# Hybrid decoder step on one core: the samples' recurrent outputs taken from the old state, the state update moved into the MLP phase

## The chip, the cores and the metric

The kernel runs on one core of a Trainium2 chip. The metric is the device time of one execution in microseconds (us). The engines are named as in the profile: PE (TensorE: matmuls), PEld (its weight loads), DVE (VectorE), ACT (ScalarE), POOL (GpSimd, which here also issues DMAs) and SP (whose queue issues the weight loads).

## What is computed

One layer of a decoder for 256 prompt rows and 8 sample rows (one new token each). A mixer with three branches (A: spatial gating, B: HGRN2 recurrence, C: gated linear attention, GLA) is followed by a squared-ReLU MLP. What the change touches is the recurrence of the 8 samples, which have a state S of 128 x dv per head (HGRN2: 8 heads, dv 128; GLA: 4 heads, dv 256):

```python
def gated_linear_recurrence(q, k, v, log_f, s0):
    """S_t = diag(f_t) S_{t-1} + k_t v_t^T ; o_t = S_t^T q_t (per head)."""
...
x = x + gt1 * rmsnorm(out, p['g_post_mix'][l])
h2 = rmsnorm(x, p['g_pre_mlp'][l]) * (1.0 + sc2) + sh2
y2 = jnp.square(jax.nn.relu(h2 @ p['w_mlp_up'][l])) @ p['w_mlp_down'][l]
x = x + gt2 * rmsnorm(y2, p['g_post_mlp'][l])
```

The updated state S_t of each sample is an output of its own; nothing else in the step reads it. The output o_t goes on into the branch's projection. Since a sample has one token, o = S_t^T q can also be had from the old state: o = S_old^T (f q) + (k.q) v.

## The kernel before

All 264 rows go through every weight matrix together. A weight block arrives by a DMA of 512 KB from SP's queue into one of four `raw` tiles (`Stream.load`), ACT casts a half of it to `whi` (L109) and DVE subtracts to make the remainder `wlo` (L106); there are six buffers of each (`SPLIT_BUFS`). PE then runs three matmuls for each 128x128 piece (`granule`, L601 to L603). A granule is 24 such matmuls and uses two `whi`/`wlo` pairs, one for each 12 matmuls; a column of 256 outputs takes four granules in the up projection of the MLP and in `zin`, two in the down projection. At the end of a column ACT or DVE takes the sum out of PSUM (two buffers, `new_acc`).

Everything else runs beside this stream. After each granule `background()` advances one tick: generators in the queue `bg` do the mixer's branches, those in `bs` the samples, each at its `rate`; `slot()` then puts the small PE matmuls that have become ready between two granules. In the mixer phase the order of PE and POOL is that of the code; DVE and ACT are ordered by a scheduler at build time, and each engine executes strictly in its order. In the MLP phase before the change only PE's order was fixed.

The samples' recurrence is `samples_r(G)`, one generator for each of the three groups (two of 4 HGRN2 heads, one of the 4 GLA heads). In its preparation it makes `fs` = f and `qm` (q of each sample, spread over columns of its own). Then, for each of 8 samples (in one step of 4 heads, or in GLA's case two steps of 2 heads):

- `fetch` (L1073) brings the old state into one of 4 `st` tiles; `values` (L1079) brings v, broadcast over the partitions, from the DRAM scratch `vs_d` into one of 2 `vbc` tiles. Both are DMAs that POOL issues;
- ACT multiplies each head by f (L1099), DVE adds k times v (L1101): `st` now is the new state;
- POOL issues its write to the output (L1102);
- `slot()` multiplies the new state by `qm` on PE (L640) and DVE adds the product up in `os` (L103).

When all samples of a group are done, `os` is normalised; `finish(i)` later transposes it into the branch's rows. Beside it `mixer_r` works on the prompt rows of the same group; its products `kd` and `qd` are read by PE at L1220.

Of the kernel before, what the change touches and what calls it, by code (L numbers as in the profile page):

```python
# [11 lines left out]
ALU = mybir.AluOpType  # L12
# [36 lines left out]
SLOT_WAIT = 4  # L49
HELD_OWED = 1.0  # L50
LEVELS_HELD = 3
FETCHED = 3
AGE = 2
ADA_LAND = 4

# [2 lines left out]
def hybrid_step_kernel(  # L58
# [39 lines left out]

    def mul(o, a, b):
        V.tensor_tensor(o, a, b, op=ALU.mult)  # L100

    def add(o, a, b):
        V.tensor_tensor(o, a, b, op=ALU.add)  # L103
# [505 lines left out]
    def slot():  # L609

        lv = [x for x in levels if x[0] + AGE <= now[0]][:2]
        if any(x[3] == 64 for x in lv):
            lv = lv[:1]
        sv = [x for x in samples if x[0] + AGE <= now[0]]
        del levels[:len(lv)]
        del samples[:len(sv)]
        pls, two = [], None
        for _, lhs, rhs, m, _ in lv:
            if m == 64:
                pl = sm([P, 8, 64])  # L620
            else:
                two = two or sm([P, 2, 8, 32])
                pl = two[:, len(pls)]
            pls.append(pl)
            n = max(m, 32)
            for h in range(4):
                for hf in range(2):
                    for b in range(4):
                        if m >= 32 and b // (n // 32) % 2:
                            continue  # L630
                        t0 = hf * P + b * 32
                        q0 = t0 if m < 32 else hf * P + b // (n // 32) * n + n
                        T.matmul(pl[32 * b:32 * b + 32, 2 * h + hf, :], lhs[:, h, t0:t0 + 32], rhs[:, h, q0:q0 + n], start=True, stop=True)  # L633
        if sv:
            G, qm, os_ = sv[0][1]
            nh = 512 // G.dv
            po = sm([P, G.dv])
            for h in range(4):
                for i, (_, _, b, sts) in enumerate(sv):
                    T.matmul(po[32 * h:32 * h + 32, :], qm[:, h, b, :], sts[h // nh][:, h % nh, :], start=i == 0, stop=i == len(sv) - 1)  # L640
        if rounds.due():
            rounds.steps()
        for pl, x in zip(pls, lv):
            x[4](pl)
        if sv:
            if sv[0][2] == 0:
                V.tensor_copy(os_, po)
            else:
                add(os_, os_, po)

    later = []

# [222 lines left out]
    def mixer_a():  # L875
# [30 lines left out]
            add(v, v, lnb)  # L906
            yield

        vs = tmp([P, 8, NS], "vsa", 1)
        w8 = tmp([P, 8, NS], "vsb", 1)  # L910
        r8 = tmp([P, NS], "vsr", 1)
        for i in range(2):
# [66 lines left out]

    att = const([P, 8, P], "att")  # L980
    nc.gpsimd.memset(att, 0.0)
    vs_d = dp.tile([3, 8 * NS, P], F32, tag="vs_d", name="vs_d")

    class Group:
# [73 lines left out]
    def samples_r(G):  # L1058

        dv = G.dv  # L1060
        nj, nh = dv // P, 512 // dv
        q, k, g = G.q, G.k, G.g
        fs = tmp([P, 4, NS], "fs")
        S.activation(fs, g[:, :, NP:NT], AF.Exp)
        qm = blk([P, 4, NS, 32])
        mul(qm, q[:, :, NP:NT].unsqueeze(3).to_broadcast([P, 4, NS, 32]),
            delta.rearrange("p (b c) -> p b c", b=NS).unsqueeze(1).to_broadcast([P, 4, NS, 32]))
        steps = [(b, h) for b in range(NS) for h in range(0, 4, nh)]
        ahead, vals = [], []

        def fetch(b, h):
            st = tmp([P, nh, dv], "st", ST_BUFS)
            nc.gpsimd.dma_start(st, G.s_in(b, h, nh))  # L1073
            ahead.append((st, now[0]))

        def values(b, h):
            v = tmp([P, 4, P], "vbc", VB_BUFS)
            r0 = 4 * nj * b + h * nj
            nc.gpsimd.dma_start(v, vs_d[G.i, r0:r0 + 4, :].partition_broadcast(P))  # L1079
            vals.append((v.rearrange("p (h j) v -> p h (j v)", h=nh), now[0]))  # L1080

        for s in steps[0:2]:
            fetch(*s)
            yield
        values(*steps[0])
        yield
        os_ = tmp([P, dv], f"os{G.i}", 1)
        sts = []
        for n, (b, h0) in enumerate(steps):
            if n + 2 < len(steps):  # L1090

                yield lambda: len(sts) + sum(len(x[3]) for x in samples) <= ST_BUFS - 3
                fetch(*steps[n + 2])
            if n + 1 < len(steps):
                values(*steps[n + 1])
            yield lambda: now[0] >= max(ahead[0][1] + FETCHED, vals[0][1] + FETCHED - 1)
            st, v = ahead.pop(0)[0], vals.pop(0)[0]
            for i in range(nh):
                S.activation(st[:, i, :], st[:, i, :], AF.Copy, scale=fs[:, h0 + i, b:b + 1])  # L1099
            for i in range(nh):  # L1100
                V.scalar_tensor_tensor(st[:, i, :], v[:, i, :], k[:, h0 + i, NP + b:NP + b + 1], st[:, i, :], ALU.mult, ALU.add)  # L1101
            nc.gpsimd.dma_start(G.s_out(b, h0, nh), st)  # L1102
            sts.append(st)
            if h0 + nh == 4:
                samples.append((now[0], (G, qm, os_), b, sts))
                sts = []
            yield
        yield lambda: not samples
        yield READY
        ss, rr = tmp([P, 1], "sss", 1), tmp([P, 1], "srr", 1)  # L1110
        S.activation(tmp([P, dv], "vt"), os_, AF.Square, accum_out=ss)
        rstd_small(ss, 1.0 / dv, rr)
        S.activation(os_, os_, AF.Copy, scale=rr)
        G.os = os_
        yield

    def mixer_r(G):
# [172 lines left out]
                yield 0.6  # L1290
        G.o = o

    def finish(i):
# [114 lines left out]
    gs = tmp([P, KT, NS], "gs", 1)  # L1408

    def gated(m, src, Gv):  # L1410

# [312 lines left out]
    def up(f, zs=()):  # L1724
        ah, al = [], []
        for m in range(FB // CW):
            z = zs[m] if m < len(zs) else linear(w_mlp_up[0], 0, KT, f * FB + m * CW, CW, h2H, h2L)
            rl = tmp([P, 2, NT], "vt")
            S.activation(rl, z, AF.Relu)  # L1729
            if m % 2 == 0:  # L1730
                ah.append(blk(dt=F32R))
                al.append(blk(dt=F32R))
            a, b = pair(ah[-1], m % 2), pair(al[-1], m % 2)
            sq = tmp([P, 2, NT], "gt")
            S.activation(a, rl, AF.Square)  # L1735
            mul(sq, rl, rl)
            sub(b, sq, a.bitcast(F32))
        return tiles(ah), tiles(al)
# [31 lines left out]
    order = tc.manual_schedule(engines={mybir.EngineType.PE})  # L1770
    order.__enter__()
    pend = up(0, zs)
    for f in range(NFB):
        nxt = up(f + 1) if f + 1 < NFB else None
        if f == NFB - 1:
            rounds.drain()
            mul(G2, mod[:, 5 * KT:6 * KT, :], gpost2T.unsqueeze(2).to_broadcast([P, KT, NC]))
# [92 lines left out]
```

## Time and profile before

| | |
|---|---|
| time before, 3 runs | median 1937.72 us, 1937.01 to 1941.59 |
| the profiled execution | 1936.48 us, of which the span of the trace is 1934.7 |
| PE, PEld busy | 1900.5 us, 1811.2 us |
| DVE, ACT, POOL busy | 1191.7 us, 996.9 us, 87.7 us |
| moved by DMA | 442.06 MB |
| samples' recurrence in the trace | from 372.9 us (first fetch) to 845.3 us (last product) |

The times lie along the program like this: start and the first pass over the input projection up to 300 us, the mixer to 1130, the change to the MLP around 1150, the MLP to 1922, and the end. In what follows, a row of the timeline has the start, the duration, the engine, the line and the operation, and in brackets the engine's idle time ahead of it with what ended it. A row of a table by stretches has, for each engine, busy time and number of instructions, then the granted PE clock (1.00 is full), the DMA engines' mean busy share and the GB/s moved.

### The profile page before, as it was taken

The page shows a single profiled execution, that of the slowest core. Times are in us where ns is not written, and L with a number is a line of the kernel's source. Part 1 is how long each engine was busy: PE and PEld are TensorE (multiplying, and loading weights), DVE is VectorE, ACT ScalarE, POOL GpSimd, SP SyncE. Part 2 cuts the span into 40 slices and gives each one's busy share as a digit, 9 for nine tenths or more (in the row PEclk, how much of TensorE's full clock was granted, in tenths as well). Part 3 has the DMA queues.
Part 4 walks back from the last instruction along what each step waited for, and adds up shares of the span by engine and source line. Part 5 has one row for each costly group of instructions (what it writes and reads, how often), then busy time and mean ns, then how long its engine had stood idle before and what let it go on. Part 6 is the DMA issues. An engine that isn't in the chain of part 4 may idle for free.

```text
span 1934.7 us, 42322 instructions
## 1 busy us (share of the span) xinstructions
PE 1900.5 (98%) x17092; PEld 1811.2 (94%) x17092; DVE 1191.7 (62%) x2129; ACT 996.9 (52%) x1812; POOL 87.7 (5%) x144
## 2 busy tenths in 40 slices
PE   7999999998999999999999999999999999999998
PEld 5989999998999998999999999999999999999997
DVE  5666567685577695565555667545555555555666
ACT  4444354664666765544444566454444545454544
POOL 1000000001101112200000010000000000000000
PEclk9999999999999999999999999999999999999999
DMA  9986696777588678987777846776655556565563
GB/s 325 349 319 236 226 307 206 226 254 252 184 269 278 221 260 277 309 264 251 251 252 231 304 143 193 230 239 188 183 178 183 182 179 184 176 184 179 181 183 102
DMA packets 339380, 442.06 MB, mean 228 GB/s; under 512 B 14930, under 2 KB 281024, under 8 KB 339184
## 3 DMA queue, kind: packets, MB, share of 16 engines
q1 hardware_dynamic: 329120, 409.62, 65.6%
q0 software_dynamic: 8992, 28.48, 4.6%
q8 instruction: 134, 2.20, 0.4%
q10 hardware_dynamic: 1072, 1.25, 0.2%
q14 instruction: 62, 0.51, 0.1%
HBM read 427.60 MB, written 11.70 MB: 227 GB/s over the span
## 4 chain that ended last, share of the span: by engine, by line
PE 94%; DVE 2%; DMA 2%; ACT 1%; issue 1%; POOL 0%; SPq 0%; DVEq 0%; ACTq 0%
PE mm L601 29%; PE mm L602 28%; PE mm L603 28%; PE ada L341 3%; PE ada L273 2%; DMA vbc<-vs_d 1%; PE sm L633 1%; DVE wlo L106 1%; PE sm L845 1%; PE sm L640 0%; DMA st<-in_state_gla_dram 0%; DMA b<-in_x_prompt_dram 0%; DVE b L103 0%; DMA b<-in_w_ada_dram 0%; ACT b L109 0%
## 5 line engine op out<-in xcount | busy, mean ns | idle before, releaser
L601 PE MATMUL mm<-b,whi 128*128 128x264 f32 x4592 | 1318.1, 287 | 5.7 <-DVE b L103 2.9
L602 PE MATMUL mm<-b,whi 128*128 128x264 f32 x4592 | 1307.7, 285 | 1.4 <-DVE b L106 1.2
L603 PE MATMUL mm<-b,wlo 128*128 128x264 f32 x4592 | 1305.1, 284 | 3.1 <-DVE wlo L106 2.6
L106 DVE TENSOR_TENSOR wlo<-raw,whi 128x512 fp32r<-128x512 f32 x1136 | 770.3, 689 | 498.0 <-ACT whi L109 495.4
L109 ACT CAST whi<-raw 128x512 fp32r<-128x512 f32 x1132 | 692.3, 618 | 726.9 <-PE mm L602 648.2
L601 PEld LDWEIGHTS mm<-b,whi 128*128 128x128 f32 x4592 | 865.4, 188 | 49.2 <-issue 24.7
L603 PEld LDWEIGHTS mm<-b,wlo 128*128 128x128 f32 x4592 | 865.5, 188 | 3.7 <-DVE wlo L106 3.7
L602 PEld LDWEIGHTS mm<-b,whi 128*128 128x128 f32 x4592 | 865.5, 188 | 2.4 <-DVE b L106 1.3
L103 DVE TENSOR_TENSOR b<-b,mm 128x528 f32<-128x528 f32 (+1 forms) x137 | 95.7, 700 | 98.2 <-PE mm L603 98.2
L1101 DVE SCALAR_TENSOR_TENSOR st<-vbc,b,st 128x128 f32<-128x128 f32 (+1 forms) x96 | 34.2, 391 | 54.7 <-DMA vbc<-vs_d 49.8
L1099 ACT ACTIVATE st<-st,fs 128x128 f32<-128x128 f32 (+1 forms) x96 | 37.0, 430 | 58.7 <-DMA st<-in_state_hgrn_dram 32.5
L273 PE MATMUL ada<-b,cT 128*32 128x256 f32 (+1 forms) x640 | 34.7, 354 | 6.9 <-DMA b<-in_w_ada_dram 6.8
L341 PE MATMUL ada<-araw,cT 128*32 128x512 f32 x296 | 39.9, 601 | 0.0
L273 PEld LDWEIGHTS ada<-b,cT 128*32 128x32 f32 x640 | 17.8, 112 | 18.8 <-ACT b L234 6.1
L100 DVE TENSOR_TENSOR b<-b,b 128x512 f32<-128x512 f32 (+1 forms) x47 | 34.1, 742 | 1.4 <-ACT b L1209 0.9
L1102 POOL DMA_DIRECT2D out_dram<-st x32 | 23.5, 735 | 156.4 <-DVE st L1101 155.6
L341 PE MATMUL ada<-b,cT 128*32 128x512 f32 x216 | 25.8, 593 | 0.0
L106 DVE TENSOR_TENSOR b<-gt,b 128x528 fp32r<-128x528 f32 x32 | 22.7, 708 | 3.6 <-ACT whi L109 0.5
L106 DVE TENSOR_TENSOR b<-b 128x1024 f32<-128x1024 f32 (+1 forms) x24 | 24.3, 1018 | 0.0
L100 DVE TENSOR_TENSOR gt<-vt 128x528 f32<-128x528 f32 x32 | 22.5, 702 | 0.9 <-ACT vt L1729 0.9
L1735 ACT ACTIVATE b<-vt 128x528 fp32r<-128x528 f32 x32 | 20.7, 647 | 1.0
L341 PEld LDWEIGHTS ada<-b,cT 128*32 128x32 f32 x216 | 6.9, 110 | 15.1 <-issue 14.6
(385 smaller groups left out, 882.6 us busy)
## 6 DMA issues: line engine op xcount, KB each, us to landing
raw<-in_w_in_dram SPq DMA_DIRECT2D x232, 512.0 KB, 4.6
raw<-in_w_mlp_up_dram SPq DMA_DIRECT2D x128, 512.0 KB, 3.7
raw<-in_w_mlp_down_dram SPq DMA_DIRECT2D x128, 512.0 KB, 3.6
b<-in_w_ada_dram SPq DMA_DIRECT2D x102, 512.0 KB, 6.3
araw<-in_w_ada_dram SPq DMA_DIRECT2D x74, 512.0 KB, 5.4
raw<-in_w_branch_dram SPq DMA_DIRECT2D x48, 512.0 KB, 4.3
raw<-in_w_out_dram SPq DMA_DIRECT2D x32, 512.0 KB, 4.2
b<-in_w_ada_dram SPq DMA_DIRECT2D x32, 256.0 KB, 6.5
```

Source lines behind the costliest of these rows:

```text
L100: V.tensor_tensor(o, a, b, op=ALU.mult)
L103: V.tensor_tensor(o, a, b, op=ALU.add)
L106: V.tensor_tensor(o, a, b, op=ALU.subtract)
L109: S.copy(hi, src)
L273: T.matmul(acc[32 * j:32 * j + 32, 0:n], cT[:, k, :], w[:, n * j:n * j + n], start=k == 0, stop=k == KT - 1)
L341: T.matmul(self.acc[32 * j:32 * j + 32, :], cT[:, k, :], ws[j // 2][:, j % 2 * 512:j % 2 * 512 + 512], start=k == 0, stop=k == KT - 1)
L601: T.matmul(o, a, xh(k + j), start=first and j == 0, stop=False)
L602: T.matmul(o, a, xl(k + j), start=False, stop=False)
L603: T.matmul(o, b, xh(k + j), start=False, stop=last and j == n - 1)
L1099: S.activation(st[:, i, :], st[:, i, :], AF.Copy, scale=fs[:, h0 + i, b:b + 1])
L1101: V.scalar_tensor_tensor(st[:, i, :], v[:, i, :], k[:, h0 + i, NP + b:NP + b + 1], st[:, i, :], ALU.mult, ALU.add)
L1102: nc.gpsimd.dma_start(G.s_out(b, h0, nh), st)
```

## The change

`samples_r` no longer updates the state. It forms f q instead of q for `qm`, multiplies the old state by it as it lands, and starts `os` with (k.q) v: v and the products k q are put into a padded tile `pads` and transposed on PE (four transposes in all), k q is summed over the partitions by one small matmul per group, and ACT scales. The fetched states rotate through the 4 `st` and the 2 `vbc` tiles; POOL issues neither `values` nor the writes in the mixer phase. f and k of all groups are kept in `kept`.

A new generator `states()` does the update in the MLP phase: it fetches each of the 32 steps' state a second time, with v beside it, and works in half steps (2 heads, or in GLA's case 1). Each half step waits until a column has been taken out of PSUM: POOL copies one element per partition of that column (the token), then the factors f and k that the half step needs, and ACT and DVE then do their operation as before. The write of a step is issued behind the next token. There are 65 tokens, one for each column from the up projection of the MLP's second block on. POOL's order is now fixed in that phase too.

```diff
-FETCHED = 3
+FETCHED = 4
+UPDATE_RATE = 9.0
...
-        fs = tmp([P, 4, NS], "fs")
+        fs, ks = (kept[:, G.i, c].rearrange("p (h b) -> p h b", h=4) for c in range(2))
...
+            odd = fetched[0] % 3 == 2
+            fetched[0] += 1
+            st = tmp([P, nh, dv], "vbc" if odd else "st", VB_BUFS if odd else ST_BUFS)
             nc.gpsimd.dma_start(st, G.s_in(b, h, nh))
...
+            T.transpose(ps, pads.rearrange("p h b -> p (h b)"), ident)
+            S.copy(os_[:, j * P:(j + 1) * P], ps)
...
+        mul(pads[:, :, 0:NS], q[:, :, NP:NT], ks)
+        mul(qf, q[:, :, NP:NT], fs)
...
+        T.matmul(ps[:, 0:1], pads.rearrange("p h b -> p (h b)"), ones[:, 0:1], start=True, stop=True)
...
+        S.activation(os_, os_, AF.Copy, scale=kq)
...
-            for i in range(nh):
-                S.activation(st[:, i, :], st[:, i, :], AF.Copy, scale=fs[:, h0 + i, b:b + 1])
-            for i in range(nh):
-                V.scalar_tensor_tensor(st[:, i, :], v[:, i, :], k[:, h0 + i, NP + b:NP + b + 1], st[:, i, :], ALU.mult, ALU.add)
-            nc.gpsimd.dma_start(G.s_out(b, h0, nh), st)
...
+        def token():
+            nc.gpsimd.tensor_copy(tmp([P, 16], "sa")[:, 0:1], paced[0])
+            paced[0] = None
...
+            for half in range(2):
+                yield lambda: paced[0] is not None
+                token()
+                hs = range(half * nh // 2, (half + 1) * nh // 2)
+                fk = tmp([P, 16], "sx")[:, 0:nh].rearrange("p (c i) -> p c i", c=2)
+                nc.gpsimd.tensor_copy(fk, kept[:, G.i].rearrange("p c (h b) -> p c h b", h=4)[:, :, h + hs[0]:h + hs[-1] + 1, b])
+                write()
+                for j, i in enumerate(hs):
+                    S.activation(st[:, i, :], st[:, i, :], AF.Copy, scale=fk[:, 0, j:j + 1])
+                    V.scalar_tensor_tensor(st[:, i, :], v[:, i, :], fk[:, 1, j:j + 1], st[:, i, :], ALU.mult, ALU.add)
+                if half == 0 and n + 1 < len(todo):
+                    fetch(*todo[n + 1])
...
             S.activation(rl, z, AF.Relu)
+            paced[0] = rl[:, 0, 0:1]
...
                     add(dst[:, i, :], dst[:, i, :], z[:, i, :])
+            paced[0] = dst[:, 0, 0:1]
```

DVE's order in the mixer phase, first group, around the last states of the group, before the change (`wlo` is a weight's remainder, L1101 the update of a state, L100 the product `qd` that PE reads at L1220):

```order
L106 TENSOR_TENSOR wlo_6084<-raw_5942,whi_6083 128x512
L1101 SCALAR_TENSOR_TENSOR st_5860<-vbc_6104,b_4817,st_5860 128x128 x3
L106 TENSOR_TENSOR wlo_6088<-raw_5942,whi_6087 128x512
L1101 SCALAR_TENSOR_TENSOR st_5860<-vbc_6104,b_4817,st_5860 128x128
L1101 SCALAR_TENSOR_TENSOR st_6102<-vbc_6115,b_4817,st_6102 128x128 x2
L106 TENSOR_TENSOR wlo_6146<-raw_5987,whi_6145 128x512
L1101 SCALAR_TENSOR_TENSOR st_6102<-vbc_6115,b_4817,st_6102 128x128
L1340 SCALAR_TENSOR_TENSOR b_5868<-gt_6056,mm_6058 128x528
L106 TENSOR_TENSOR wlo_6150<-raw_5987,whi_6149 128x512
L1101 SCALAR_TENSOR_TENSOR st_6102<-vbc_6115,b_4817,st_6102 128x128
L106 TENSOR_TENSOR wlo_6182<-raw_6021,whi_6181 128x512
L100 TENSOR_TENSOR b_6094<-b_6094,b_581 128x512
```

The same place after the change (L107 and L101 are the old L106 and L100, L104 the old L103, L1395 the old L1340):

```order
L107 TENSOR_TENSOR b_6051<-b_656 128x1024
L104 TENSOR_TENSOR os_888_5109<-os_888_5109,sm_5994 128x128
L101 TENSOR_TENSOR b_6051<-b_6051,b_4818 128x1024
L107 TENSOR_TENSOR wlo_6042<-raw_5903,whi_6041 128x512
L101 TENSOR_TENSOR b_6052<-b_6052,b_581 128x512
L107 TENSOR_TENSOR wlo_6046<-raw_5903,whi_6045 128x512
L107 TENSOR_TENSOR wlo_6089<-raw_5941,whi_6088 128x512
L1395 SCALAR_TENSOR_TENSOR b_5827<-gt_6014,mm_6016 128x528
```

The updates are gone from between the weights' remainders, and the product that PE reads at L1220 stands right behind the first remainder instead of behind eight updates and four remainders of later blocks.

POOL's order for the same group before the change, from the fourth fetch (`st` from the input is a fetch, `vbc` the values, `out_dram` a write):

```order
L1073 DMA st_5460<-in_state_hgrn_dram 128x4x128
L1079 DMA vbc_5462<-vs_d 128x512
L1102 DMA out_dram<-st_5108 128x4x128
L1073 DMA st_5607<-in_state_hgrn_dram 128x4x128
L1079 DMA vbc_5609<-vs_d 128x512
L1102 DMA out_dram<-st_5306 128x4x128
L1073 DMA st_5847<-in_state_hgrn_dram 128x4x128
L1079 DMA vbc_5849<-vs_d 128x512
```

And after it, the whole group (L1073 is the fetch in both):

```order
L1073 DMA st_5105<-in_state_hgrn_dram 128x4x128
L1073 DMA st_5107<-in_state_hgrn_dram 128x4x128
L1080 MEMSET xsn_5110 128x128
L1073 DMA vbc_5588<-in_state_hgrn_dram 128x4x128
L1073 DMA st_5624<-in_state_hgrn_dram 128x4x128
L1073 DMA st_5660<-in_state_hgrn_dram 128x4x128
L1073 DMA vbc_5821<-in_state_hgrn_dram 128x4x128
L1073 DMA st_5869<-in_state_hgrn_dram 128x4x128
L1073 DMA st_5907<-in_state_hgrn_dram 128x4x128
```

Values no longer stand behind a fetch that waits for a free tile; eight fetches are left, and nothing on DVE or ACT waits for any of them.

DVE's order in the MLP's down projection after the change (L104 takes a column out of PSUM, L1340 is the update; before, there was the same without the rows of L1340):

```order
L107 TENSOR_TENSOR wlo_17596<-raw_17481,whi_17595 128x512
L104 TENSOR_TENSOR b_14892<-b_14892,mm_17523 128x528
L107 TENSOR_TENSOR wlo_17600<-raw_17481,whi_17599 128x512
L1340 SCALAR_TENSOR_TENSOR st_17252<-vbc_17253,sx_17643,st_17252 128x128 x2
L107 TENSOR_TENSOR wlo_17632<-raw_17515,whi_17631 128x512
L107 TENSOR_TENSOR wlo_17636<-raw_17515,whi_17635 128x512
L107 TENSOR_TENSOR wlo_17674<-raw_17556,whi_17673 128x512
L104 TENSOR_TENSOR b_14892<-b_14892,mm_17606 128x528
```

A half step stands once in each column, one remainder behind the column's evacuation; the three remainders behind it wait in DVE's queue for it.

More of the change, by code (lines that the diff above doesn't have):

```diff
@@ L1090, in samples_r @@
             if n + 2 < len(steps):
[L1092 removed]
+                yield lambda: len(sts) + sum(len(x[3]) for x in samples) <= ST_BUFS - 1
                 fetch(*steps[n + 2])
[L1094 to L1097, printed above, removed]
[L1098 to L1103 removed]
+            yield lambda: now[0] >= ahead[0][1] + FETCHED
+            sts.append(ahead.pop(0)[0])
             if h0 + nh == 4:
@@ L1291, in mixer_r, with states, fetch, write @@
         G.o = o
+    paced = [None]
+    def states():
+        todo = [(G, b, h) for G in Gs for b in range(NS) for h in range(0, 4, 512 // G.dv)]
+        ahead, done = [], []
+        def fetch(G, b, h):
+            nj, nh = G.dv // P, 512 // G.dv
+            st, v = tmp([P, nh, G.dv], "st", ST_BUFS), tmp([P, 4, P], "vbc", VB_BUFS)
+            nc.gpsimd.dma_start(st, G.s_in(b, h, nh))
+            r0 = 4 * nj * b + h * nj
+            nc.gpsimd.dma_start(v, vs_d[G.i, r0:r0 + 4, :].partition_broadcast(P))
+            ahead.append((st, v.rearrange("p (h j) v -> p h (j v)", h=nh)))
+        def token():
+            nc.gpsimd.tensor_copy(tmp([P, 16], "sa")[:, 0:1], paced[0])
+            paced[0] = None
+        def write():
+            while done:
+                nc.gpsimd.dma_start(*done.pop(0))
+        yield lambda: paced[0] is not None
+        token()
+        fetch(*todo[0])
+        for n, (G, b, h) in enumerate(todo):
+            nh = 512 // G.dv
+            st, v = ahead.pop(0)
+            for half in range(2):
+                yield lambda: paced[0] is not None
+                token()
+                hs = range(half * nh // 2, (half + 1) * nh // 2)
[7 more added lines that the diff above has]
+                    fetch(*todo[n + 1])
+            done.append((G.s_out(b, h, nh), st))
+        yield lambda: paced[0] is not None
+        token()
+        write()
     def finish(i):
@@ L1769, in hybrid_step_kernel @@
     order.__exit__(None, None, None)
-    order = tc.manual_schedule(engines={mybir.EngineType.PE})
+    order = tc.manual_schedule(engines={mybir.EngineType.PE, mybir.EngineType.Pool})
     order.__enter__()
     pend = up(0, zs)
+    bs.g.append(states())
+    paced[0] = None
+    rate[:] = (0.0, UPDATE_RATE)
     for f in range(NFB):
```

47 lines of the change are left out of this document (28 added, 19 removed).

## The prediction

> **What bounds the kernel now.** The page comes first.
>
> ```profile
> span 1934.7 us, 42322 instructions
> PE 1900.5 (98%) x17092; PEld 1811.2 (94%) x17092; DVE 1191.7 (62%) x2129; ACT 996.9 (52%) x1812; POOL 87.7 (5%) x144
> ```
>
> PE is busy for all but 34.2 us. A change that leaves the matmuls as they are can win no more than what PE idles where the change works, and what PE does more slowly there. So I read PE by stretches: the mixer with the samples in it, then the part of the MLP that gets the update.
>
> ```profile
> core 0: us, PE busy (x) PEld busy (x) DVE busy (x) ACT busy (x) POOL busy (x), PEclk, DMA share, GB/s
> ...
> 440.00:484.00 44.00, 38.23 (x471) 35.40 (x471) 24.57 (x49) 21.05 (x45) 8.15 (x12) 0.92 0.79 251
> 484.00:660.00 176.00, 175.48 (x1908) 164.22 (x1904) 115.83 (x243) 117.92 (x260) 18.63 (x28) 1.00 0.73 234
> 660.00:815.00 155.00, 154.93 (x1653) 144.17 (x1653) 106.98 (x185) 97.08 (x192) 28.43 (x43) 1.00 0.85 281
> ...
> 1207.00:1350.00 143.00, 143.00 (x1171) 135.70 (x1170) 73.44 (x109) 69.61 (x117) 0.00 (x0) 1.00 0.69 221
> 1350.00:1726.00 376.00, 376.00 (x3094) 376.00 (x3093) 217.80 (x322) 176.70 (x290) 0.00 (x0) 1.00 0.60 181
> ```
>
> Only the first row has something to give: PE idles 44 - 38.23 = 5.77 us in it, and its clock is at 0.92. The second group (484 to 660) and the GLA group idle half a microsecond or less. In the MLP PE does not idle at all; 376 us for 3094 instructions is 0.1215 us each, so 12 matmuls (one `whi`/`wlo` pair) take 1.46 us and a down column of 48 takes 5.83.
>
> Which waits make up the 5.77 us, the list of waits and the timeline of PE say:
>
> ```profile
> PE sm L1220 <- DVE b L100: 3.8, 1, 3.8
> PE mm L603 <- DVE wlo L106: 2.6, 4, 1.9
> ```
>
> ```profile
> 454.62 0.28 PE L602 MATMUL mm<-b,whi 128*128 128x264 f32 x1
> 456.81 0.39 PE L603 MATMUL mm<-b,wlo 128*128 128x264 f32 x1 [1.91 <-DVE wlo L106]
> ...
> 459.19 0.42 PE L601 MATMUL mm<-b,whi 128*128 128x264 f32 x1
> 459.41 0.42 PE L602 MATMUL mm<-b,whi 128*128 128x264 f32 x1
> ...
> 477.75 1.24 PE L1220 MATMUL sm<-b,b 128*128 128x128 f32 x8 [3.84 <-DVE b L100]
> ```
>
> Two gaps, 1.91 and 3.84 us, both behind DVE. Between 459.19 and 459.41 matmuls start 0.22 us apart rather than 0.12: after a gap PE runs at half speed for a while. The clock of the two stretches prices that:
>
> ```profile
> 456.00:464.00 8.00, 7.17 (x86) 0.79 0.51 145
> 476.00:484.00 8.00, 6.25 (x57) 0.79 0.77 255
> ```
>
> Each loses (1 - 0.79) x 8 = 1.68 us, together 3.36. The two gaps cost 5.77 + 3.36 = 9.13 us.
>
> Why was DVE late? Its own timeline, and POOL's:
>
> ```profile
> 446.51 0.69 DVE L106 TENSOR_TENSOR wlo<-raw,whi 128x512 fp32r<-128x512 f32 x1 [2.48 <-ACT whi L109]
> 454.92 0.61 DVE L1101 SCALAR_TENSOR_TENSOR st<-vbc,b,st 128x128 f32<-128x128 f32 x2 [7.71 <-DMA vbc<-vs_d]
> ```
>
> ```profile
> 443.71 0.75 POOL L1073 DMA_DIRECT2D st<-in_state_hgrn_dram  x1 [16.07 <-PE sm L640]
> 444.45 0.55 POOL L1079 DMA_DIRECT2D vbc<-vs_d  x1
> ```
>
> POOL stood 16.07 us at a fetch for which no `st` tile was free; the values queued behind it were issued only at 444.45, and DVE stood 7.71 us at L1101 with the weights' remainders behind it. That is head-of-line blocking on two engines in a row. The backlog lasts to the second gap: DVE's order puts eight updates ahead of the product that L1220 needs.
>
> **The change part by part.** *Update out of the mixer.* DVE and ACT lose L1101 and L1099 there, with these waits:
>
> ```profile
> DVE st L1101 <- DMA vbc<-vs_d: 49.8, 18, 7.7
> ACT st L1099 <- DMA st<-in_state_hgrn_dram: 32.5, 9, 7.1
> ```
>
> After it no instruction of DVE or ACT waits for a samples' DMA in the mixer, and POOL has one kind of DMA left. Both gaps lose their cause: -9.13 us. Next late would be the remainder's own chain, ACT's cast and DVE's subtraction, which has kept PE fed elsewhere in the mixer (0.07 us idle in 155, at a DMA share of 0.85).
>
> *States read by PE directly.* A product now waits on PE for its fetch. By the order there are at least six granules of 2.92 us, 17.5 us, between a fetch and its product. The tile view of `vbc`, which has the same size of 256 KB, has the landing times:
>
> ```profile
> DMA to landing us min/median/max: 3.7/6.5/11.3
> ```
>
> So 6 us are left at the worst landing: cost 0. If the cover went, PE would wait and lose a half-speed stretch as well; a rival below prices that. The Trainium skill (DMA: Bandwidth & Descriptors, section Anatomy of one DMA) fits 2.0 us plus the bytes at 436 GB/s, an estimate of 2.6 us for 256 KB; the trace's 6.5 differs and decides, and by the page this cover would only be thicker.
>
> *Added on PE.* Four transposes and three one-column sums, each alone between two granules. The nearest row is the single transpose at L865:
>
> ```profile
> 368.93 0.28 PE L603 MATMUL mm<-b,wlo 128*128 128x264 f32 x1
> 369.05 0.27 PE L865 MATMUL sm<-cst,srow 128*128 128x128 f32 x1
> 369.08 0.36 PE L601 MATMUL mm<-b,whi 128*128 128x264 f32 x1
> 369.28 0.28 PE L602 MATMUL mm<-b,whi 128*128 128x264 f32 x1
> ```
>
> From L603 to L602 it is 0.35 us where two matmuls take 0.24: 0.11 each, seven make +0.8. Against that the order has 66 interruptions of PE by 32-column matmuls instead of 68. A lone group of such products costs at most this:
>
> ```profile
> 838.28 0.28 PE L603 MATMUL mm<-b,wlo 128*128 128x264 f32 x1
> 838.50 0.64 PE L640 MATMUL sm<-st,b 128*32 128x256 f32 x8
> 839.06 0.39 PE L601 MATMUL mm<-b,whi 128*128 128x264 f32 x1
> ```
>
> That is 0.78 from start to start, 0.66 over the usual 0.12, but its eight matmuls still run in another group. Two fewer are worth 0 to 1.3 us; I take 0.6, the middle. The new small copies, products and scalings on DVE and ACT (fewer than ten each per group, against 32 updates removed from each) hide in the time given back.
>
> *The update in the MLP.* 64 half steps. Without the waits each is two L1099 on ACT and two L1101 on DVE:
>
> ```profile
> L1099 ACT ACTIVATE st<-st,fs 128x128 f32<-128x128 f32 x64 | 21.9, 393 | 32.6 <-DMA st<-in_state_hgrn_dram 32.5
> L1101 DVE SCALAR_TENSOR_TENSOR st<-vbc,b,st 128x128 f32<-128x128 f32 x64 | 19.4, 347 | 27.5 <-DMA vbc<-vs_d 27.4
> ```
>
> A down column has 5.83 us. DVE does four remainders, one evacuation and now a half step in it; the first two are seen here:
>
> ```profile
> 1456.75 0.70 DVE L103 TENSOR_TENSOR b<-b,mm 128x528 f32<-128x528 f32 x1 [0.22 <-PE mm L603]
> 1457.37 0.69 DVE L106 TENSOR_TENSOR wlo<-raw,whi 128x512 fp32r<-128x512 f32 x1
> ```
>
> 4 x 0.69 + 0.70 + 2 x 0.35 = 4.16 us, and the new wait: DVE stands at L1101 until token, factor copy and the first ACT scaling are through, with three remainders queued behind it. POOL's nearest rows are its 128x32 casts, four in a mean of 0.49 us (2.0 us in all):
>
> ```profile
> L1642 POOL CAST b<-xsn 128x32 fp32r<-128x32 f32 x4 | 2.0, 488 | 0.1
> ```
>
> Two copies, 0.98, and ACT's 0.39 make 1.4; 0.69 of it passes beside the remainder ahead of L1101. DVE waits about 0.7 us and uses 4.9 of 5.83. A late remainder doesn't reach PE: with six buffers, one is remade when PE lets it go and read five pairs later, 5 x 1.46 = 7.3 us, less a cast and a subtraction some 5.9 us of slack. An up column has twice the time. Fetch and values are issued two columns (11.7 us) ahead, a landing of 11.3 at worst. The 25 MB moved here (three times 256 KB for 32 steps) over 519 us add 48 GB/s to 181 to 221, at most 281 in a down column beside the other loads, the rate at which the GLA stretch ran without gaps. Cost 0; weight loads in SP's queue are the next to be late if that cover fails.
>
> Here the Trainium skill (SBUF — State Buffer, Reading the diagram) speaks against the change: a GpSimd instruction that reads SBUF and a VectorE one with two SBUF inputs exclude each other for their whole length. By it 130 copies of 0.49 us would take up to 64 us of DVE's 519, an estimate; at 56% busy with 9% of updates that still leaves room, and no run here yet shows the copies.
>
> Sum: 1936.48 - 9.13 + 0.8 - 0.6 = 1927.6 for the profiled execution (span 1934.7, 1.8 around it). The median of the runs lies 1.24 above, so **1928.8 us**, -0.46%.
>
> **The rivals.** *Half steps become the bound of the down columns (slower).* If the chain token, copy, ACT lasts so long that DVE waits over 5.83 - 4.16 = 1.67 us a column, each column is late by the rest, and PE stalls once the slack is used. At 2.4 us, with both copies held up by a remainder of 0.69 and a landing that is late, about 40 down half steps lose 0.73 each: 29 - 5.9 = 23 us, so 1937.7 - 8.9 + 23 = 1952. For it: three remainders stand behind each wait. Against: 0.7 by the rows, and DVE under 60% busy.
>
> *PE waits for a state (half the gain).* If a landing under load exceeds 17.5 us once, PE gets a gap of some 2.7 us and a half-speed stretch of 1.7: about 1933. Against: 11.3 is the longest seen.
>
> *The gaps stay (no change).* ACT's and DVE's other work around 450 to 480, the copies of `att` and the products of two levels, could be late without the updates as well: 1937.7. Against: 7.71 us of one wait precedes the first gap, and the second has eight updates ahead of it.
>
> **How the numbers follow.** The forecast has 0.66, half the gain 0.14, no change 0.08, slower 0.12. About 0.3% (5.8 us) is what can be told from no change: faster is below 1931.9, so 0.66; same is 0.14 + 0.08 = 0.22; slower 0.12. Range: its low end is all of 9.13, the 0.52 of the next stretch, the full 1.3 and 0.7 for the spread of the runs below their median (1937.72 - 9.13 - 0.52 - 1.3 + 0.8 - 0.7), 1926.9; the high end takes in half the gain with a second such wait, 1936.0. That leaves out no change and slower, 0.2.
>
> **What would show it.** Right: no PE idle over 1 us and a clock of 1.00 from 400 to 500 us; POOL without a wait of 16 us there; from about 1200 to 1720 us some 130 short copies on POOL, DVE's waits at the update under 1.7 us, PE busy throughout. Wrong: PE waits on `wlo` or `whi` in the down columns, or on a state's DMA at L640, or gaps that stay at L1220.

## The result, and the profile after

The changed kernel takes 1927.79 us (median of 6 runs, 1927.26 to 1930.37), the kernel before 1935.95 us (6 runs, 1933.97 to 1941.59, the three of the table among them). The ratio is 0.9958, interval 0.9947 to 0.9969: 0.42% faster, where 0.46% was forecast. The profiled execution is the slowest of the six, 1930.37 us. Its page:

```profile
span 1928.6 us, 42604 instructions
PE 1903.9 (99%) x17102; PEld 1815.4 (94%) x17102; DVE 1202.5 (62%) x2143; ACT 1005.4 (52%) x1819; POOL 154.5 (8%) x309
```

PE is busy 3.4 us longer in a span that is 6.1 us shorter, so it idles 24.7 us instead of 34.2. The table by stretches, over the same stretches as before:

```profile
440.00:484.00 44.00, 44.00 (x568) 41.69 (x567) 25.73 (x49) 22.86 (x43) 1.50 (x2) 1.00 0.65 201
484.00:660.00 176.00, 176.00 (x1891) 165.57 (x1890) 109.24 (x203) 112.09 (x228) 8.42 (x13) 1.00 0.70 218
660.00:815.00 155.00, 155.00 (x1666) 142.51 (x1666) 100.95 (x175) 86.86 (x168) 13.96 (x21) 1.00 0.75 243
...
1207.00:1350.00 143.00, 143.00 (x1172) 135.70 (x1171) 80.59 (x137) 78.03 (x145) 23.83 (x54) 1.00 0.82 260
1350.00:1726.00 376.00, 376.00 (x3091) 376.00 (x3091) 241.87 (x390) 199.41 (x357) 81.98 (x169) 1.00 0.75 232
```

In the first row PE went from 38.23 to 44.00 us and its clock from 0.92 to 1.00; both gaps are gone. In the last two rows PE is as full as before, although DVE and ACT have the updates and POOL the copies in them.

Where along the program the time is won is seen best from instructions that both kernels have at the same place. The first and last start of the single transposes (L845, now L843) and of the up columns' evacuation (L1729, now L1784), before:

```profile
L845 PE MATMUL sm<-cst,b x48: 271/272/310, 307.8 to 658.6; 128*128 128x128 f32 x48
L845 PE MATMUL sm<-cst,gt x60: 270/272/329, 1060.7 to 1922.3; 128*128 128x128 f32 x60
L1729 ACT ACTIVATE vt<-mm x32: 602/607/612, 1180.3 to 1824.5; 128x528 f32<-128x528 f32 x32
```

and after:

```profile
L843 PE MATMUL sm<-cst,b x48: 271/272/309, 308.4 to 654.2; 128*128 128x128 f32 x48
L843 PE MATMUL sm<-cst,gt x60: 270/272/329, 1051.2 to 1913.5; 128*128 128x128 f32 x60
L1784 ACT ACTIVATE vt<-mm x32: 605/606/614, 1170.8 to 1815.6; 128x528 f32<-128x528 f32 x32
```

At 308 us this execution is 0.6 behind the one before, at 1051 it is 9.5 ahead: the mixer gives 10.1 us. From the first to the last up column it takes 644.8 instead of 644.2 us: 0.6 is lost. At the last up column it is 8.9 ahead, at the end 6.1 (the spans). The end ran at a clock of 0.78 in this execution, 0.93 in the one before (from the last weight matmul on), which takes those 2.8 us back; by the medians the change wins 8.2.

In the MLP a down column now looks like this, DVE, ACT and POOL in turn:

```profile
1353.56 0.70 DVE L104 TENSOR_TENSOR b<-b,mm 128x528 f32<-128x528 f32 x1 [0.25 <-PE mm L604]
1354.18 0.69 DVE L107 TENSOR_TENSOR wlo<-raw,whi 128x512 fp32r<-128x512 f32 x1
1355.50 0.64 DVE L1340 SCALAR_TENSOR_TENSOR st<-vbc,sx,st 128x128 f32<-128x128 f32 x2 [0.64 <-ACT st L1339]
```

```profile
1355.06 0.70 ACT L1339 ACTIVATE st<-st,sx 128x128 f32<-128x128 f32 x2 [1.02 <-POOL sx L1336]
```

```profile
1354.39 0.51 POOL L1318 COPY sa<-b 128x1 f32<-128x1 f32 x1 [2.68 <-DVE b L104]
1354.85 0.18 POOL L1336 COPY sx<-kept 128x4 f32<-128x4 f32 x1
```

The chain is as the change has it: evacuation, token, factors, ACT, DVE. DVE stands 0.64 us. The list of waits has 41 of the 64 half steps, and no such wait for the others:

```profile
DVE st L1340 <- ACT st L1339: 28.6, 41, 0.7
```

28.6 / 41 = 0.70 us, never more than 0.7. The landings of the refetched states and of the values took 4.1 to 8.4 and 5.1 to 8.8 us, and no engine waited for one.

### The profile page after: what moved, and what is told of

Read it like the earlier page. It is cut to its first block, busy times and chain, and to the rows that moved or that the text cites. A ratio compares the mean times of both kernels' runs of the same rounds, so it can differ in the third digit from the quotient of the medians.

```text
span 1928.6 us, 42604 instructions
## 1 busy us (share of the span) xinstructions
PE 1903.9 (99%) x17102; PEld 1815.4 (94%) x17102; DVE 1202.5 (62%) x2143; ACT 1005.4 (52%) x1819; POOL 154.5 (8%) x309
## 4 chain that ended last, share of the span: by engine, by line
PE 96%; DVE 1%; ACT 1%; DMA 1%; issue 0%; SPq 0%; ACTq 0%; DVEq 0%
PE mm L602 29%; PE mm L603 29%; PE mm L604 28%; PE ada L342 3%; PE ada L274 2%; PE sm L634 1%; PE sm L843 1%; PE sm L641 1%; DVE wlo L107 1%; DMA b<-in_x_prompt_dram 0%; DVE b L104 0%; DMA b<-in_w_ada_dram 0%; ACT b L110 0%; PE sm L261 0%; PE mm L1856 0%
## 5 line engine op out<-in xcount | busy, mean ns | idle before, releaser
L107 DVE TENSOR_TENSOR wlo<-raw,whi 128x512 fp32r<-128x512 f32 x1136 | 773.8, 690 | 498.9 <-ACT whi L110 495.5
L104 DVE TENSOR_TENSOR b<-b,mm 128x528 f32<-128x528 f32 (+1 forms) x137 | 95.7, 700 | 98.7 <-PE mm L604 98.6
L1339 ACT ACTIVATE st<-st,sx 128x128 f32<-128x128 f32 (+1 forms) x96 | 39.3, 434 | 37.2 <-POOL sx L1336 37.2
L1340 DVE SCALAR_TENSOR_TENSOR st<-vbc,sx,st 128x128 f32<-128x128 f32 (+1 forms) x96 | 36.1, 394 | 28.6 <-ACT st L1339 28.6
L1318 POOL COPY sa<-vt 128x1 f32<-128x1 f32 x24 | 16.8, 700 | 296.7 <-ACT vt L1784 296.7
L274 PEld LDWEIGHTS ada<-b,cT 128*32 128x32 f32 x640 | 18.0, 114 | 18.9 <-issue 6.5
L101 DVE TENSOR_TENSOR b<-b,b 128x512 f32<-128x512 f32 (+1 forms) x47 | 34.0, 742 | 1.7 <-ACT b L1218 0.9
L1318 POOL COPY sa<-b 128x1 f32<-128x1 f32 x42 | 19.0, 451 | 179.7 <-DVE b L104 142.8
L107 DVE TENSOR_TENSOR b<-gt,b 128x528 fp32r<-128x528 f32 x32 | 22.7, 709 | 3.3
L107 DVE TENSOR_TENSOR b<-b 128x1024 f32<-128x1024 f32 (+1 forms) x24 | 24.4, 1018 | 0.0
L101 DVE TENSOR_TENSOR gt<-vt 128x528 f32<-128x528 f32 x32 | 22.5, 702 | 0.9 <-ACT vt L1784 0.9
```

Source lines behind the costliest of these rows:

```text
L107: V.tensor_tensor(o, a, b, op=ALU.subtract)
L274: T.matmul(acc[32 * j:32 * j + 32, 0:n], cT[:, k, :], w[:, n * j:n * j + n], start=k == 0, stop=k == KT - 1)
L1318: nc.gpsimd.tensor_copy(tmp([P, 16], "sa")[:, 0:1], paced[0])
L1339: S.activation(st[:, i, :], st[:, i, :], AF.Copy, scale=fk[:, 0, j:j + 1])
L1340: V.scalar_tensor_tensor(st[:, i, :], v[:, i, :], fk[:, 1, j:j + 1], st[:, i, :], ALU.mult, ALU.add)
```

## The experiments

The theory: before, DVE and ACT stood at updates whose DMAs had not landed, with the weights' remainders queued behind; these waits and nothing else cost the time. In the MLP the update is free because it waits little and PE has slack. The rivals: the update's arithmetic itself was too much for the mixer; its DMA traffic was; POOL's order alone was to blame; the update does cost something in the MLP.

**The order of POOL alone.** In the kernel before, values ahead of the blocked fetch:

```diff
+            if n + 1 < len(steps):
+                values(*steps[n + 1])
             if n + 2 < len(steps):
                 yield lambda: len(sts) + sum(len(x[3]) for x in samples) <= ST_BUFS - 3
                 fetch(*steps[n + 2])
-            if n + 1 < len(steps):
-                values(*steps[n + 1])
```

> The kernel before, with one swap: in each step of the samples the values of the next step are issued ahead of the fetch of the state after it, so that they no longer stand behind a fetch that waits for a free tile. The update stays in the mixer. My theory (head-of-line blocking in POOL's queue makes DVE late): the wait of 7.7 us at the update and the PE gap of 1.9 us at 457 go; the second gap (3.8 us) goes too if it is backlog of the first wait. Time 1927 to 1929, -0.35 to -0.45%. Rival A (the updates themselves crowd DVE, eight of them ahead of the product that L1220 reads): the second gap stays, about 5.5 us with its half-speed stretch, so only 3.6 us are won: 1932. Rival B (it isn't POOL's order at all): 1936, no change.

Measured: 1940.98 us against 1937.14 before, ratio 1.0019 (1.0010 to 1.0029): a little slower. PE's waits in the mixer (372 to 850 us), before and in this run:

```profile
PE sm L1220 <- DVE b L100: 3.8, 1, 3.8
PE mm L603 <- DVE wlo L106: 2.1, 2, 1.9
```

```profile
PE mm L603 <- DVE wlo L106: 2.3, 3, 1.5
PE sm L1220 <- DVE b L100: 2.1, 1, 2.1
PE sm L633 <- DVE b L100: 1.7, 1, 1.7
PE sm L1242 <- ACT b L1233: 1.6, 1, 1.6
```

The DVE wait of 7.7 us is gone, the gap at 457 is down to 0.2 and the second gap is shorter, but there are new ones at 569, 589 and 756. DVE still waits for the values, 34.8 us in 14 times (49.8 in 18 before), and ACT for the states. There is less waiting of DVE and ACT for DMAs, and yet PE's four waits above add up to 7.7 us where the two of before make 5.9. By the starts of the same weight matmuls in both traces the swap wins 4.1 us between 447 and 493 us and loses 5.8 from there to 860. So the expectation was wrong: the values' place in POOL's queue chose where a gap fell, not whether there was one. How much of the 3.8 us is the swap's own isn't shown: 1.4 of what this execution loses falls at 417 to 427 us, ahead of the gaps, and 1.5 behind the mixer, where its clock is at 0.57 from 1149 to 1153 us.

**Arithmetic or waits.** Two kernels from the one before. The first leaves the update's arithmetic out:

```diff
-            for i in range(nh):
-                S.activation(st[:, i, :], st[:, i, :], AF.Copy, scale=fs[:, h0 + i, b:b + 1])
-            for i in range(nh):
-                V.scalar_tensor_tensor(st[:, i, :], v[:, i, :], k[:, h0 + i, NP + b:NP + b + 1], st[:, i, :], ALU.mult, ALU.add)
```

> The kernel before without the arithmetic of the update: ACT's scaling and DVE's multiply-add of each state are left out, so the states go out as they came in; all fetches, values, writes and products stay. My theory (PE is late only because DVE and ACT stand at the update with the weights' remainders behind it): both gaps go, 9 us, 1927 (the DMA traffic of before stays in the mixer and costs nothing). Rival (the traffic of values and writes in the mixer delays weights or states, not the queue order): gaps in 440 to 484 stay in part, 1931 to 1936.

The second keeps it, on a tile of its own that no DMA fills; it leaves the transfer of values out, and the states go out as they came in:

```diff
+        own = tmp([P, 4, P], "vbc", VB_BUFS)
+        nc.gpsimd.memset(own, 0.0)
...
-            v = tmp([P, 4, P], "vbc", VB_BUFS)
-            nc.gpsimd.dma_start(v, vs_d[G.i, r0:r0 + 4, :].partition_broadcast(P))
+            v = own
...
-                S.activation(st[:, i, :], st[:, i, :], AF.Copy, scale=fs[:, h0 + i, b:b + 1])
+                S.activation(v[:, i, :], v[:, i, :], AF.Copy, scale=fs[:, h0 + i, b:b + 1])
...
-                V.scalar_tensor_tensor(st[:, i, :], v[:, i, :], k[...], st[:, i, :], ALU.mult, ALU.add)
+                V.scalar_tensor_tensor(v[:, i, :], v[:, i, :], k[...], v[:, i, :], ALU.mult, ALU.add)
```

> The kernel before, whose update does its 64+64 small and 32+32 larger operations of ACT and DVE on a scratch tile of its own instead of on the fetched state: as much arithmetic on both engines in the mixer as before, but nothing in it waits for a DMA (the transfer of values is left out, the states go out as they came in). By its order the operations stand closer together than before, up to nine updates of DVE in a row (3.1 us). My theory (the waits for the samples' DMAs with remainders queued behind them cost the 9 us, not the 27 and 31 us of arithmetic): no gap over 1 us from 440 to 480 us, 1927 to 1930. Rival (the arithmetic itself crowds DVE and ACT past PE's slack): gaps behind the runs of updates, 1932 to 1938.

Measured: 1928.08 us without the arithmetic (ratio 0.9947, 0.9933 to 0.9961) and 1927.68 with all of it but no wait (0.9942, 0.9924 to 0.9961). The stretch of the two gaps, first without the arithmetic:

```profile
440.00:484.00 44.00, 44.00 (x566) 40.69 (x565) 24.14 (x40) 23.21 (x41) 8.14 (x12) 1.00 0.86 275
```

and with arithmetic and no wait:

```profile
440.00:484.00 44.00, 44.00 (x566) 40.70 (x565) 24.64 (x39) 22.59 (x41) 5.97 (x8) 1.00 0.77 253
```

PE is full in both. The first moved 275 GB/s there, more than the 251 of before, so traffic wasn't it; the second had the arithmetic, bunched closer than before (up to nine updates in a row on DVE instead of seven), and 253 GB/s beside it, so neither was it arithmetic, nor both together. The wait was. A caution: taking the wait away also let the build-time scheduler place the updates earlier, so this run has another order on DVE; PE's order is that of before.

The second run prices the waits, too. Its two landmarks:

```profile
L845 PE MATMUL sm<-cst,b x48: 271/273/310, 308.7 to 648.9; 128*128 128x128 f32 x48
L845 PE MATMUL sm<-cst,gt x60: 270/272/329, 1050.4 to 1912.5; 128*128 128x128 f32 x60
```

From the first to the second it is 1050.4 - 308.7 = 741.7 us, where the kernel before took 1060.7 - 307.8 = 752.9: 11.2 us, of which 9.6 fall between 447 and 493 us (by the starts of the same weight matmuls in both traces), 0.7 at 580 and 0.6 at 832. The other 0.3, at 420 us, may be chance: executions of kernels that have the same code up to there differ by up to 0.7 at this place.

**What the update costs in the MLP.** The changed kernel without the generator of the MLP phase (no second fetch, no half steps, no states' outputs):

```diff
-    bs.g.append(states())
```

> The changed kernel with the generator of the MLP phase left out: no second fetch, no tokens, no half steps, and the states' outputs are not written. It is the mixer's gain alone. My theory (the update is free where it now stands, since PE has 5.9 us of slack and DVE about 0.9 us of room per down column): the same as the changed kernel within 1 us, 1927 to 1928. Rival (the update costs something in the MLP, by the extra 8 MB each way, by DVE's waits or by the clock): 2 to 5 us faster than the changed kernel, 1923 to 1926.

Measured: 1927.42 us (1926.82 to 1928.33), 0.4 from the changed kernel.

```profile
L1784 ACT ACTIVATE vt<-mm x32: 604/605/614, 1170.6 to 1815.4; 128x528 f32<-128x528 f32 x32
```

1815.4 - 1170.6 = 644.8 us, the same as with the update. The 0.6 us that the changed kernel loses there to the one before is thus not the update's. What it is wasn't looked for.

**How much room there is.** The factors' copy repeated, 6 and 15 times in all:

```diff
-                nc.gpsimd.tensor_copy(fk, kept[...])
+                for _ in range(6):
+                    nc.gpsimd.tensor_copy(fk, kept[...])
```

> The changed kernel, with POOL's copy of the factors made six times instead of once before each half step (the same values into the same place). Five more copies of 0.18 us make the chain ahead of each half step about 0.9 us longer, so DVE waits 1.6 instead of 0.7 us at the update. My theory (a down column has room for a wait of 1.67 us, and PE another 5.9 us of slack behind it): just under the limit, no cost, within 1 us of the changed kernel, 1927 to 1929. Rival (there is no such room; what DVE waits, PE loses in each of some 40 down columns): +30 us or more. A second rival (copies on GpSimd hold up the two-input operations of DVE, 320 copies of 0.18 us): the remainders' mean rises over 0.69 us, and some us are lost.

> The same with fourteen more copies, 2.55 us, so that DVE waits about 3.2 us at each half step. My theory: 1.6 us over the limit in each down column; a stretch of 8 down columns falls behind by 12.6 us, of which the slack takes 5.9, so about 6.7 us are lost in each of five such stretches, while the up columns between (room of 4.0 us, 1.4 left) win back some 6: +25 to +35 us, 1953 to 1963, with PE waiting for remainders or casts in the second half of each down stretch only. Rival (the chain doesn't reach PE, the wait is off the path): 1928.

Measured: 1928.76 us (1928.21 to 1930.86) and 1989.84 us (1988.14 to 1991.82): nothing that can be told from none, and 62 us. DVE's wait at the update and PE's busy time with five copies more:

```profile
DVE st L1341 <- ACT st L1340: 75.6, 64, 1.9
```

```profile
1350.00:1726.00 376.00, 376.00 (x3091) 376.00 (x3090) 238.35 (x388) 194.90 (x355) 161.07 (x414) 1.00 0.76 231
```

and with fourteen, DVE's and then PE's waits and POOL's copies:

```profile
DVE st L1341 <- ACT st L1340: 223.0, 59, 4.1
```

```profile
PE mm L602 <- ACT whi L110: 31.2, 28, 1.4
PE mm L604 <- DVE wlo L107: 7.0, 32, 0.2
```

```profile
L1337 POOL COPY sx<-kept 128x2 f32<-128x2 f32 x365 | 86.0, 236 | 20.7
```

With five, the wait is 75.6 / 64 = 1.2 us, under the 1.67 that the prediction put as the limit, and PE stays full. With fourteen it is 223.0 / 59 = 3.8 us and PE stalls. The direction is as expected, the size is twice: a copy took 0.24 us and not 0.18, so the wait was 3.8 and not 3.2. That is 2.1 over the limit in each of some 40 down columns, 84 us; the slack takes 5.9 of it once, and the 24 up columns, whose room of 4.0 is nearly used up, give back 0.2 each and not the 6 between two stretches that were expected: 73 by this sum, against 62. The weight matmuls' starts show it column by column: PE falls 1.6 to 2.1 us behind in seven of the eight down columns of each of the last four stretches, and 5.9 us in the first stretch, 59 us in all. So a column cost 1.9 on average, not 2.1, and the first one of a stretch was free. The stop shows first at ACT's casts, which wait in ACT's queue behind the scaling just as the remainders do in DVE's. The second rival, copies that hold up DVE, did not come: over the same columns the remainder's mean is 690 ns with five copies more and 687 with fourteen, 691 before.

**The token.** The changed kernel without POOL's copy of the evacuated column:

```diff
-            nc.gpsimd.tensor_copy(tmp([P, 16], "sa")[:, 0:1], paced[0])
             paced[0] = None
```

> The changed kernel without POOL's copy of the evacuated column: half steps are issued at the same places of the program, but nothing releases them, so the build-time scheduler sets them into DVE's and ACT's order as early as it likes; by the order all 64 stand among 88 remainders (128 us of PE) instead of 339. A step then has 4.0 us, while its tiles have 2 buffers for values and a landing of some 6.4 us plus the update's 1.5, so about 4 us a step at the best and 5 at a rate with weights beside it. My theory (the release matters, because a half step that DVE meets before its DMA has landed blocks the remainders): 10 to 40 us slower than the changed kernel, 1938 to 1968, with PE waiting for remainders between 1140 and 1300 us. Rival (the release is needless, PE's slack covers any order): 1927 to 1929.

Measured: 1979.02 us, ratio 1.0217 (1.0201 to 1.0234), 51 us over the changed kernel. The updates in the tile view, the stretch, and DVE's longest wait:

```profile
L1339 DVE SCALAR_TENSOR_TENSOR st<-vbc,sx,st x96: 339/351/486, 1141.1 to 1337.6; 128x128 f32<-128x128 f32 x64, 128x256 f32<-128x256 f32 x32
```

```profile
1140.00:1340.00 200.00, 166.68 (x1200) 152.95 (x1193) 112.20 (x231) 107.25 (x235) 92.38 (x169) 0.92 0.85 275
```

```profile
DVE st L1339 <- DMA vbc<-vs_d: 66.6, 20, 7.3
```

All updates are crowded into 196.5 us, 6.1 a step; DVE stands at values that have not landed, PE idles 33.3 us of 200 and its clock falls to 0.92. It is the fault of before, larger and in another place. The step time was set too low in the expectation (4 to 5 us), hence 51 and not 10 to 40.

**The cover of the states that PE reads.** Fetches without lookahead, and in a second kernel products issued as soon as a sample is complete:

```diff
-FETCHED = 4
+FETCHED = 0
...
-        for s in steps[0:2]:
-            fetch(*s)
...
-            if n + 2 < len(steps):
-                fetch(*steps[n + 2])
+            if n + 0 < len(steps):
+                fetch(*steps[n + 0])
```

and in the second kernel also

```diff
-                samples.append((now[0], (G, qm, os_), b, sts))
+                samples.append((now[0] - AGE, (G, qm, os_), b, sts))
```

> The changed kernel with the samples' states fetched without any lookahead in the mixer: by the order 2 to 5 granules (5.8 to 14.6 us) lie between a fetch and its product, two in three cases and three in half of them, where the changed kernel has 6 at least. Landings of such transfers took 3.1 to 9.3 us, 6.4 in the median. My theory (only the cover hides the landing; an uncovered one stalls PE and costs a half-speed stretch of 1.7 us besides): PE waits for a state's DMA at the product's line some one to five times, 0.5 to 3.5 us each, 1930 to 1936 in all. Rival (a landing is hidden anyway, since PE's weight queue and the slot's other products come first): 1928.

> The changed kernel with the states fetched without lookahead, as in the run with the late fetch, and the products issued as soon as a sample is complete: by the order 0 to 3 granules between a fetch and its product, none in 8 cases and one in 9. It prices the cover that the changed kernel has. My theory (PE stands for what is left of a landing of about 6.4 us, and runs at half speed for some 1.7 us after each such stop): about ten products wait 3.5 to 6.4 us each, 5 to 8 with the half-speed stretch, +50 to +80 over the changed kernel, 1978 to 2008, with PE's waits put down to the states' DMAs. Rival (such a landing is hidden by the transposes and other products of the slot): under 1935.

Measured: 1931.35 us (1930.61 to 1933.74, ratio 0.9971, 0.9960 to 0.9981) and 1931.77 us (1930.69 to 1934.74, ratio 0.9974, 0.9963 to 0.9985). The first lies in the expected range, the second far under its 1978 to 2008 and where its rival put it (under 1935), and the reason fell in both: PE is idle for no state, and a single weight load of a product waits for one, 0.45 us in the second kernel. POOL's timeline of the first group says why. The changed kernel:

```profile
373.72 1.57 POOL L1073 DMA_DIRECT2D st<-in_state_hgrn_dram  x2
...
377.63 0.78 POOL L1073 DMA_DIRECT2D vbc<-in_state_hgrn_dram  x1
444.06 1.50 POOL L1073 DMA_DIRECT2D st<-in_state_hgrn_dram  x2 [65.65 <-PE sm L641]
```

and the kernel with no lookahead and immediate products:

```profile
372.98 1.57 POOL L1073 DMA_DIRECT2D st<-in_state_hgrn_dram  x2
...
376.74 0.77 POOL L1073 DMA_DIRECT2D vbc<-in_state_hgrn_dram  x1
444.67 1.49 POOL L1073 DMA_DIRECT2D st<-in_state_hgrn_dram  x2 [67.16 <-PE sm L641]
```

They are the same: POOL has nothing to wait for but free tiles, runs through six fetches at once and is some 65 us ahead of the first product. Where tiles are free, a fetch's place in the program sets no time. In the third group that doesn't hold. There POOL also stands at writes of the prompt rows' outputs, with the fetches queued behind them, and in the second kernel one state lands only when its product is due:

```profile
741.76 0.73 POOL L1254 DMA_DIRECT2D out_dram<-b  x1 [25.03 <-DVE b L104]
...
744.54 0.72 POOL L1073 DMA_DIRECT2D vbc<-in_state_gla_dram  x1
```

```profile
750.31 0.14 PEld L641 LDWEIGHTS sm<-vbc,b 128*32 128x32 f32 x4 [0.45 <-DMA vbc<-in_state_gla_dram]
```

With fetches and products taken in their order, the shortest time from a landing to its first product is 24.0 us in the changed kernel, 7.0 without lookahead and 0.0 with immediate products. So the lookahead does give cover; even without it nearly all landings were still hidden.

The 3.6 and 4.0 us that these two kernels lose are something else. PE shows hardly any idle time for them (0.4 and 0.6 us from 360 to 860); the time in which it does other matmuls between the weights' (360 to 860 us, from one weight matmul's start to the next) is 92.2 us in the changed kernel, 94.0 and 96.1 in these, so about half of the first loss and all of the second lie in how the products are grouped. Why one grouping costs more wasn't settled. The first kernel's other half lies behind the mixer: between 1134 and 1144 us its clock is 0.83, where the changed kernel has 1.00 with the same idle time, and it falls 1.7 us behind. That this comes from the edit isn't shown; the run with arithmetic and no wait loses as much there. What a landing that is uncovered by more than 0.45 us costs PE stays untried.

## Why the prediction was right, point by point

- *Both gaps go, -9.13.* Right in place and cause: PE idles 0 of 44 us and the clock is 1.00. The waits were worth more than the two idle times and half-speed stretches, 11.2 us by the run with arithmetic and no wait. Some of it lies outside the stretch that was priced (0.7 and 0.6, and the 0.3 that may be chance), and the 9.6 inside are 0.5 more.
- *The cause of the late DVE.* Half right. That updates waiting for DMAs held up remainders is shown by the two runs on arithmetic. That the values' place behind the blocked fetch was the root is not: when they were moved ahead of it, other waits came in its place.
- *PE's additions, +0.8 - 0.6.* Too small. The mixer's gain is 10.1 of 11.2, so the additions and the new grouping of the products cost about 1.1 us where 0.2 was put. That and the larger gain cancel in part: -8.9 forecast for the mixer, -10.1 measured, and 0.6 lost in the MLP, for which the sum has no term. That the total came so near (-8.9 forecast, -8.2 by the medians) is partly luck.
- *States read by PE, cost 0.* Right, and with more to spare than it says: "at least six granules", 17.5 us, were read from the program's order, but the shortest time from a fetch to its product was 27.8 us, with landings of 9.3 at most, since POOL fetches ahead wherever tiles are free, some 65 us in the first group. For the same reason the sign "POOL without a wait of 16 us" did not come: it waits 65.65 us, and nobody behind it minds.
- *The update in the MLP, cost 0.* Right, with the terms of the chain: a wait of 0.7 forecast and 0.70 measured, landings under 11.3, traffic of 232 to 260 GB/s under the 281 of the bound (which is the GLA stretch's rate; the sum there gives 229 to 269), 130 copies: 64 of factors and 66 tokens, one token more than was counted. The limit of 1.67 us lies between the 1.2 that cost nothing and the 3.8 that cost 62 us.
- *The rivals.* No change and half the gain are out: no gap stayed, PE waited for no state. The slower one is real, but needs a wait of over 1.67 us, and fourteen more copies were needed to show it.

## What to carry to other kernels

An instruction that waits for a DMA costs little itself; what is queued behind it on its engine costs. Put such work where the engine has room and hold it back with a token until its data must be there, then the queue never stands long; without the token the scheduler pulls it forward and it stands again. A prefetch's cover counted in program order was a lower bound here; what the transfer really gets depends on what the engine that issues it waits for, free tiles and whatever stands ahead in its queue.

## What the runs showed of the hardware

- *GpSimd's copies waited for VectorE's two-input instructions, and VectorE paid nothing.* A copy of one element per partition takes 0.18 us where VectorE's remainder has 0.10 left when it starts:

```profile
1261.16 0.18 POOL L1318 COPY sa<-b 128x1 f32<-128x1 f32 x1 [5.57 <-ACT b L1809]
```

In the down column shown above the token began 0.21 us into a remainder and took 0.51: it ended at 1354.90, 0.03 after the remainder (1354.18 + 0.69). The Trainium skill (SBUF — State Buffer, section Reading the diagram) says that whichever of the two starts first holds the ports for its whole instruction; the trace agrees where VectorE starts first (56 of the 66 tokens took 0.51 to 0.75 us). The other way round no row shows it: with five copies more, 13 remainders began 0.02 to 0.15 us into a copy of 0.19, as soon after their release as the others (0.02), and took 0.69 to 0.71. The estimate of up to 64 us of DVE's time did not come: the remainder's mean is the same before and after, over the same 376 us:

```profile
L106 DVE TENSOR_TENSOR wlo<-raw,whi 128x512 fp32r<-128x512 f32 x258 | 178.2, 691 | 148.8 <-ACT whi L109 148.8
```

```profile
L107 DVE TENSOR_TENSOR wlo<-raw,whi 128x512 fp32r<-128x512 f32 x258 | 178.2, 691 | 102.1 <-ACT whi L110 101.2
```

- *A busy PE can lose time.* In the run with fourteen more copies PE's idle time between 1207 and 1790 us is 38 us, but the weight matmuls' starts fall 60 us behind. A matmul's row is 0.28 us long and the next may start 0.12 after it, so a stall of up to 0.16 us leaves no idle time in the profile, and a longer one shows 0.16 less; 38 is a lower bound. Of the other 22 us up to 4.5 may be no stall: three stretches of 3.41 us, from 1387, 1411 and 1503 us, ran at half the clock.
- *The clock didn't follow every gap.* The gaps of 1.91 and 3.84 us before, and one of 2.12 in the run with the values first (clock 0.79 from 475 to 483 us), each had a half-speed stretch behind them. The gaps of 1.49, 1.74 and 1.55 us in that run had none: the clock is 1.00 in the 8 us from 569, 589 and 756 us. And the half-speed stretch near 1140 us in the kernel without lookahead stands where the changed kernel has the same idle time and a clock of 1.00. So a gap plus 1.7 us is the right price for the two gaps that went, but no rule for others.
